# Moving layer norm's sums, differences and squares to GpSimd, in among the attention blocks of an encoder layer

## The chip, the cores and the metric

One Trainium2 chip; the kernel runs on one of its cores. The core has a matrix engine (PE, its weight loads shown as PEld), a vector engine (DVE), a scalar engine (ACT), GpSimd (POOL) and a sync engine (SP), which here only issues DMAs. Each engine works through its own queue of instructions strictly in order, and waits on semaphores for the others. The metric is the device time of one execution in microseconds (us); lower is better.

## The reference

One layer of a hybrid encoder on 512 tokens with 1024 channels, in float32. Three parts of it matter here:

```python
h = rmsnorm(x, norm1_g); z = h @ w_in               # conv input | q | k | v | two branch gates
u = a * sigmoid(b)                                  # GLU of the conv input
u = depthwise_conv31(u) + dw_b
mu = mean(u, channels); var = mean((u - mu) ** 2)   # layer norm over the 1024 channels of a token
conv_out = silu((u - mu) * rsqrt(var + EPS) * ln_g + ln_b) @ w_pw
attn_out = windowed_gqa(q, k, v, sink) @ w_o        # 16 heads, 4 key heads, blocks of 128 queries
x = x + (gate_A * conv_out + gate_B * attn_out) @ w_out
x = x + peer_ffn(rmsnorm(x))                        # top-16 of 128 x 128 experts, 8 heads
```

The last line takes most of the time (from about 500 us on), and the change doesn't touch it.

## The kernel before, in words

Activations lie with channels on the partitions: a matrix of 1024 channels by 512 tokens is eight tiles of 128x512, such as `cv[:, k, :]`, the result of the convolution. A sum over channels is therefore a sum over partitions and over the eight tiles: PE makes it by multiplying with a 128x128 matrix of 1/1024 (`ones`), eight matmuls that add up in one PSUM tile (L360 for the mean, L368 for the variance). These are plain float32 matmuls, which the profile shows as two passes each, so 16 passes for a sum.

All other matrix products run on rounded pairs. `split` (L57 to L59) makes from a float32 tile a rounded `hi` on ACT and the residual `lo = src - hi` on DVE or POOL, and `mm3` (L61 to L66) multiplies hi by hi, hi by lo and lo by hi. A weight block of 1024x128 is loaded by SP to `wraw` and split in two halves of 128x512 (`halves`, L107 to L114), into a ring of four halves. `lo_engine` says who makes the residuals: POOL for the input projection, DVE for `w_o` (L387) and `w_pw` (L425).

The stretch around the change, in order of the program:

1. The convolution (`conv`, L224 to L233) on DVE, while PE computes the input projection.
2. Attention (L350 to L355): four key heads `g` by four query blocks `b`, so 16 blocks `attend(g, b)` (L276 to L321). A block is a chain over the engines: scores on PE; mask, bias and row maximum on DVE (L290); the negated maximum `nm` (L293) and `es` (L295) on DVE; exponentials on ACT (L298, L300); the denominator `den` (L301), its reciprocal (L303) and the scaling, half of it on DVE (L308) and half on ACT (L306); transposes on PE (L313); the split of the transposed weights on ACT and DVE; the product with v on PE; and the split of its result. The projection of a branch gate (`fill`, L332) is put in behind five of the blocks, to give PE work.
3. Layer norm (L356 to L377): sum, mean, then for each tile difference (DVE, L365), square (ACT, L367) and sum (PE, L368), then square root on ACT, reciprocal on DVE (L371), scaling (DVE, L373), `Silu` on ACT (L375), split (ACT, DVE).
4. The output projection of attention, `w_o`, eight blocks of 24 matmuls (L386 to L388), then `w_pw` (L424 to L429), then `w_out` (L410 to L416), whose first half's residuals `olo` are POOL's.

The framework's scheduler writes the instructions of each engine into one fixed order, by its own costs. So parts 2 to 4 overlap: matmuls of `w_o` stand on PE between the last attention blocks, and the layer norm begins before attention ends. An engine doesn't pass over an instruction that waits.

Of the kernel before, what the change touches and what calls it, by code (L numbers as in the profile page):

```python
# [7 lines left out]
F32 = mybir.dt.float32  # L8
# [4 lines left out]
AF = mybir.ActivationFunctionType  # L13
OP = mybir.AluOpType
# [3 lines left out]
P = 128  # L18
S = 512
D = 1024  # L20
NT = S // P
KD = D // P
# [23 lines left out]
def encoder_block(ctx, tc, x, g1, w_in, taps, dwb, lng, lnb, w_pw, sink, w_o, w_out, g2, g2row,  # L46
                  w_query, keys, ut, u, v, gfin, out):
    nc = tc.nc
    ACT, DVE, POOL, PE, SP = nc.scalar, nc.vector, nc.gpsimd, nc.tensor, nc.sync
# [20 lines left out]
    ones = const.tile([P, P], F32, name="ones")  # L70
# [4 lines left out]
    epst = const.tile([P, 1], F32, name="epst")  # L75
# [42 lines left out]
    with ExitStack() as fc:  # L118
# [13 lines left out]
        cv = cpool.tile([P, KD, S], F32, name="cv")  # L132

        with ExitStack() as x0c:
# [6 lines left out]
            with tc.manual_schedule(engines=ordered):  # L141
# [15 lines left out]
                for t in range(NT):  # L157
                    rs = sm.tile([P, 1], F32, name="rs")
# [3 lines left out]
                for k in range(KD):  # L162
# [6 lines left out]
                    if k in (1, 4):  # L169
                        n = KD // 2  # L170
# [17 lines left out]
        def proj(src, rhs, ws=None, lo_engine=POOL, ps=None):  # L188
            ws = ws or weights(src, lo_engine)
            ps = psm.tile([P, S], F32, name="mm") if ps is None else ps  # L190
            mm3(ps, ws, rhs)
            return ps
# [5 lines left out]
        with ExitStack() as ac:  # L198
# [39 lines left out]
            for i in range(2):  # L238
                ps = proj(w_in[24 + i], hT)
# [5 lines left out]
            for i in range(2):  # L245
                ps = proj(w_in[26 + i], hT)
# [85 lines left out]
            def fill(n):  # L332
                for _ in range(n):
                    gate(gates.pop(0))
# [12 lines left out]
            fill(2)  # L347
            glup.close()
            pso = ac.enter_context(tc.tile_pool(name="pso", bufs=1, space=PSUM))
            for g in range(4):  # L350
                make_bias(g)
                for b in range(NT):
                    attend(g, b)
                    if b == 1 or (g, b) == (0, 3):
                        fill(1)  # L355
            lnp = ac.enter_context(tc.tile_pool(name="lnp", bufs=2))  # L356
            ac_hi, ac_lo = bigtile(), bigtile()
            mu_ps = pso.tile([P, S], F32, name="ln")
            for k in range(KD):
                PE.matmul(mu_ps, ones, cv[:, k, :], start=k == 0, stop=k == KD - 1)  # L360
            mu = lnp.tile([P, S], F32, name="rs", bufs=1)
            ACT.activation(mu, mu_ps, AF.Copy)
            var = pso.tile([P, S], F32, name="ln")
            for k in range(KD):
                DVE.tensor_tensor(cv[:, k, :], cv[:, k, :], mu, op=OP.subtract)  # L365
                sq = lnp.tile([P, S], F32, name="sq")
                ACT.activation(sq, cv[:, k, :], AF.Square)  # L367
                PE.matmul(var, ones, sq, start=k == 0, stop=k == KD - 1)  # L368
            rs = lnp.tile([P, S], F32, name="rs", bufs=1)
            ACT.activation(rs, var, AF.Sqrt, bias=epst)  # L370
            DVE.reciprocal(rs, rs)  # L371
            for k in range(KD):
                DVE.tensor_tensor(cv[:, k, :], cv[:, k, :], rs, op=OP.mult)  # L373
                act = lnp.tile([P, S], F32, name="act", bufs=2)
                ACT.activation(act, cv[:, k, :], AF.Silu, scale=vec["lng"][:, k:k + 1],  # L375
                               bias=vec["lnb"][:, k:k + 1])
                split(ac_hi[:, k, :], ac_lo[:, k, :], act, DVE)  # L377
            acT = [(ac_hi[:, k, :], ac_lo[:, k, :]) for k in range(KD)]
            oT = [(qh[:, k, :], ql[:, k, :]) for k in range(KD)]
# [4 lines left out]

            sigmoid(1)
            for j in range(KD):  # L386
                ps = proj(w_o[j], oT, lo_engine=DVE)  # L387
                DVE.tensor_tensor(sg[1][:, j, :], ps, sg[1][:, j, :], op=OP.mult)  # L388
            sigmoid(0)

# [33 lines left out]
        for j in range(KD):  # L424
            ps = proj(w_pw[j], acT, lo_engine=DVE)  # L425
# [44 lines left out]
    with ExitStack() as rc:  # L470
# [72 lines left out]
        with qc:  # L543
# [44 lines left out]
            for h in range(HP):  # L588
                scs = []
                for p in range(2):  # L590
                    n = 2 * h + p
# [272 lines left out]
```

## Time and profile before

| | us |
|---|---|
| median of 3 runs (lowest, highest) | 1784.65 (1777.46, 1793.43) |
| the profiled execution, its own time | 1791.42 |
| its span, first to last instruction | 1789.6 |
| mean granted PE clock, as a share of full speed | 0.99 |
| PE busy | 1726.0 (96%) |
| DVE busy | 1416.6 (79%) |
| ACT busy | 769.0 (43%) |
| POOL busy | 938.3 (52%) |

The busy shares are averages over stages with different limits: POOL is at 52% over the span, but it is idle for most of attention and for most of the output projections. What the change is worth has to be read in its own stretch, from about 228 us (the end of the convolution) to about 472 us (the start of `w_out`). From there on the order of the instructions is the same in both kernels, on every engine.

A busy PE in these views isn't PE at its peak: ends of matmuls are modelled, and an instruction that waits in the pipeline counts as busy. The spacing of matmuls is the better measure.

### The profile page before, as it was taken

The page shows a single profiled execution, that of the slowest core. Times are in us where ns is not written, and L with a number is a line of the kernel's source. Part 1 is how long each engine was busy: PE and PEld are TensorE (multiplying, and loading weights), DVE is VectorE, ACT ScalarE, POOL GpSimd, SP SyncE. Part 2 cuts the span into 40 slices and gives each one's busy share as a digit, 9 for nine tenths or more (in the row PEclk, how much of TensorE's full clock was granted, in tenths as well). Part 3 has the DMA queues.
Part 4 walks back from the last instruction along what each step waited for, and adds up shares of the span by engine and source line. Part 5 has one row for each costly group of instructions (what it writes and reads, how often), then busy time and mean ns, then how long its engine had stood idle before and what let it go on. Part 6 is the DMA issues. An engine that isn't in the chain of part 4 may idle for free.

```text
span 1789.6 us, 25354 instructions
## 1 busy us (share of the span) xinstructions
PE 1726.0 (96%) x8873; PEld 1487.9 (83%) x8873; DVE 1416.6 (79%) x2507; ACT 769.0 (43%) x1379; POOL 938.3 (52%) x741
## 2 busy tenths in 40 slices
PE   7999999989999979999999999999999999998998
PEld 5788876658888868998999999999999898996776
DVE  5999956674536999999668978888878798888964
ACT  4333367882343335665433334333332333332343
POOL 4444421020134444445447878888876878886401
PEclk9999999999999989999999999999999999998999
DMA  4223210034243114988788898998898889889952
GB/s 159 86 91 99 93 57 24 25 93 144 81 140 110 57 54 136 283 259 277 273 271 313 320 320 307 328 327 313 316 320 288 290 322 331 301 300 330 352 199 93
DMA packets 158159, 379.43 MB, mean 212 GB/s; under 512 B 12544, under 2 KB 64784, under 8 KB 158032
## 3 DMA queue, kind: packets, MB, share of 16 engines
q1 hardware_dynamic: 120048, 241.21, 39.0%
q0 software_dynamic: 37120, 134.52, 22.0%
q10 hardware_dynamic: 864, 2.10, 0.3%
q8 instruction: 69, 1.13, 0.3%
q14 instruction: 58, 0.48, 0.1%
HBM read 346.84 MB, written 30.93 MB: 211 GB/s over the span
## 4 chain that ended last, share of the span: by engine, by line
PE 57%; DVE 12%; DMA 11%; issue 4%; POOL 2%; ACT 2%; SPq 0%; POOLq 0%; DVEq 0%; ACTq 0%
PE acc L65 6%; PE acc L66 6%; PE acc L64 6%; PE hps L66 6%; PE hps L65 6%; PE hps L64 6%; DMA uraw<-in_ut_dram 5%; PE mm L66 5%; PE mm L64 5%; PE mm L65 5%; DMA row<-in_v_dram,eidx 4%; DMA vraw<-in_v_dram 2%; POOL row L663 1%; POOL ulo L59 1%; DVE oij L635 1%
## 5 line engine op out<-in xcount | busy, mean ns | idle before, releaser
L59 POOL TENSOR_TENSOR ulo<-uraw,uhi 128x512 fp32r<-128x512 f32 x256 | 396.3, 1560 | 297.9 <-ACT uhi L58 288.6
L64 PE MATMUL hps<-big,uhi 128*128 128x384 f32 x1024 | 348.0, 340 | 2.2 <-ACT hb L466 2.1
L66 PE MATMUL hps<-big,ulo 128*128 128x384 f32 x1024 | 348.2, 340 | 1.2 <-POOL ulo L59 1.2
L65 PE MATMUL hps<-big,uhi 128*128 128x384 f32 x1024 | 346.7, 339 | 0.0
L66 PE MATMUL acc<-vhl,pl 128*128 128x512 f32 x768 | 303.1, 395 | 10.3 <-DVE pl L59 10.3
L64 PE MATMUL acc<-vhl,ph 128*128 128x512 f32 x768 | 302.2, 393 | 4.3 <-ACT vhl L58 3.5
L65 PE MATMUL acc<-vhl,ph 128*128 128x512 f32 x768 | 302.9, 394 | 1.1 <-DVE vhl L59 0.9
L59 POOL TENSOR_TENSOR wlo<-wraw,whi 128x512 fp32r<-128x512 f32 x120 | 157.8, 1319 | 196.0 <-ACT whi L58 190.2
L670 DVE SCALAR_TENSOR_TENSOR row<-row,h2tok 128x1024 f32<-128x1024 f32 x128 | 194.0, 1516 | 62.6 <-DMA row<-in_u_dram,eidx 62.1
L681 DVE SCALAR_TENSOR_TENSOR yacc<-row,dots,yacc 128x1024 f32<-128x1024 f32 x127 | 198.8, 1566 | 50.9 <-DMA row<-in_v_dram,eidx 50.2
L58 ACT ACTIVATE vhl<-vraw 128x1024 fp32r<-128x1024 f32 x128 | 135.2, 1056 | 241.5 <-DMA vraw<-in_v_dram 234.2
L58 ACT ACTIVATE uhi<-uraw 128x512 fp32r<-128x512 f32 x256 | 156.9, 630 | 163.3 <-PE hps L65 99.8
L64 PEld LDWEIGHTS hps<-big,uhi 128*128 128x128 f32 x1024 | 193.8, 189 | 6.3 <-ACT hb L466 2.4
L65 PEld LDWEIGHTS hps<-big,uhi 128*128 128x128 f32 x1024 | 194.0, 189 | 4.0
L66 PEld LDWEIGHTS hps<-big,ulo 128*128 128x128 f32 x1024 | 193.7, 189 | 2.7 <-POOL ulo L59 2.7
L663 POOL DMA_INDIRECT row<-in_v_dram,eidx x128 | 165.4, 1292 | 56.9 <-DVE yacc L681 32.8
L58 ACT ACTIVATE whi<-wraw 128x512 fp32r<-128x512 f32 x152 | 95.1, 631 | 231.9 <-PE mm L65 127.1
L663 POOL DMA_INDIRECT row<-in_u_dram,eidx x128 | 175.3, 1369 | 31.8 <-issue 23.8
L66 PEld LDWEIGHTS acc<-vhl,pl 128*128 128x128 f32 x768 | 145.8, 190 | 44.7 <-DVE pl L59 13.8
L59 DVE TENSOR_TENSOR vhl<-vraw,vhl 128x1024 fp32r<-128x1024 f32 x128 | 160.4, 1253 | 26.3 <-ACT vhl L58 26.1
L64 PEld LDWEIGHTS acc<-vhl,ph 128*128 128x128 f32 x768 | 145.6, 190 | 32.7 <-ACT vhl L58 3.8
L65 PEld LDWEIGHTS acc<-vhl,ph 128*128 128x128 f32 x768 | 145.6, 190 | 28.9 <-DVE vhl L59 1.8
(231 smaller groups left out, 3111.4 us busy)
## 6 DMA issues: line engine op xcount, KB each, us to landing
uraw<-in_ut_dram SPq DMA_DIRECT2D x128, 512.0 KB, 6.7
vraw<-in_v_dram SPq DMA_DIRECT2D x128, 512.0 KB, 6.0
gates_dram<-st SPq DMA_DIRECT2D x12, 2048.0 KB, 8.6
gt<-gates_dram SPq DMA_DIRECT2D x96, 256.0 KB, 6.0
wraw<-in_w_in_dram SPq DMA_DIRECT2D x44, 512.0 KB, 3.3
wraw<-in_w_query_dram SPq DMA_DIRECT2D x16, 512.0 KB, 3.4
wraw<-in_w_o_dram SPq DMA_DIRECT2D x8, 512.0 KB, 3.2
oraw<-in_w_out_dram SPq DMA_DIRECT2D x16, 256.0 KB, 3.0
```

The costliest lines, as they stand in the source:

```text
L58: ACT.activation(hi, src, AF.Copy)
L59: lo_engine.tensor_tensor(lo, src, f(hi), op=OP.subtract)
L64: PE.matmul(ps, wh, mh, start=first and i == 0, stop=False)
L65: PE.matmul(ps, wh, ml, start=False, stop=False)
L66: PE.matmul(ps, wl, mh, start=False, stop=last and i == n - 1)
L635: DVE.tensor_tensor(prs(oij), iota8, rows(0), op=OP.is_equal)
L663: POOL.indirect_dma_start(out=row, out_offset=None, in_=table, in_offset=bass.IndirectOffsetOnAxis(ap=eidx[:, c:c + 1], axis=0))
L670: DVE.scalar_tensor_tensor(row, row, 1.0, h2tok, op0=OP.mult, op1=OP.mult, accum_out=dots[:, c:c + 1])
L681: DVE.scalar_tensor_tensor(yacc, row, dots[:, c:c + 1], yacc, op0=OP.mult, op1=OP.add)
```

## The change

The layer norm's sum over tiles is made on POOL (seven additions into `stat`, L360 and L362 of the new kernel), so that PE has one column sum left of eight matmuls (`colsum`); so has the variance. Difference, square and sum of squares of each tile are three POOL instructions (`ln_square`, L366 to L370), 23 in all, since the first square goes to `stat` directly. They are called behind the attention blocks: the mean behind the second block, the squares of the eight tiles behind blocks (1,0) to (2,3). The second column sum, square root, reciprocal, scaling and `Silu` stand behind attention in the program, as before. The residuals of `w_o` are made by POOL instead of DVE (16 instructions of 128x512).

```diff
@@ -347,30 +347,44 @@
             pso = ac.enter_context(tc.tile_pool(name="pso", bufs=1, space=PSUM))
+            lnp = ac.enter_context(tc.tile_pool(name="lnp", bufs=2))
+            stat = lnp.tile([P, S], F32, name="stat", bufs=1)
+            mu = lnp.tile([P, S], F32, name="mu", bufs=1)
+
+            def colsum():
+                ps = pso.tile([P, S], F32, name="ln")
+                PE.matmul(ps, ones, stat, start=True, stop=True)
+                return ps
+
+            def ln_mean():
+                POOL.tensor_tensor(stat, cv[:, 0, :], cv[:, 1, :], op=OP.add)
+                for k in range(2, KD):
+                    POOL.tensor_tensor(stat, stat, cv[:, k, :], op=OP.add)
+                ACT.activation(mu, colsum(), AF.Copy)
+
+            def ln_square(k):
+                POOL.tensor_tensor(cv[:, k, :], cv[:, k, :], mu, op=OP.subtract)
+                sq = stat if k == 0 else lnp.tile([P, S], F32, name="sq", bufs=2)
+                POOL.tensor_tensor(sq, cv[:, k, :], cv[:, k, :], op=OP.mult)
+                if k:
+                    POOL.tensor_tensor(stat, stat, sq, op=OP.add)
+
             for g in range(4):
                 make_bias(g)
                 for b in range(NT):
                     attend(g, b)
                     if b == 1 or (g, b) == (0, 3):
                         fill(1)
-            lnp = ac.enter_context(tc.tile_pool(name="lnp", bufs=2))
+                    if (g, b) == (0, 1):
+                        ln_mean()
+                    n = 4 * g + b - 4
+                    if 0 <= n < KD:
+                        ln_square(n)
             ac_hi, ac_lo = bigtile(), bigtile()
-            mu_ps = pso.tile([P, S], F32, name="ln")
+            ACT.activation(mu, colsum(), AF.Sqrt, bias=epst)
+            DVE.reciprocal(mu, mu)
             for k in range(KD):
-                PE.matmul(mu_ps, ones, cv[:, k, :], start=k == 0, stop=k == KD - 1)
-            mu = lnp.tile([P, S], F32, name="rs", bufs=1)
-            ACT.activation(mu, mu_ps, AF.Copy)
-            var = pso.tile([P, S], F32, name="ln")
-            for k in range(KD):
-                DVE.tensor_tensor(cv[:, k, :], cv[:, k, :], mu, op=OP.subtract)
-                sq = lnp.tile([P, S], F32, name="sq")
-                ACT.activation(sq, cv[:, k, :], AF.Square)
-                PE.matmul(var, ones, sq, start=k == 0, stop=k == KD - 1)
-            rs = lnp.tile([P, S], F32, name="rs", bufs=1)
-            ACT.activation(rs, var, AF.Sqrt, bias=epst)
-            DVE.reciprocal(rs, rs)
-            for k in range(KD):
-                DVE.tensor_tensor(cv[:, k, :], cv[:, k, :], rs, op=OP.mult)
+                DVE.tensor_tensor(cv[:, k, :], cv[:, k, :], mu, op=OP.mult)
                 act = lnp.tile([P, S], F32, name="act", bufs=2)
@@ -384,7 +398,7 @@
             for j in range(KD):
-                ps = proj(w_o[j], oT, lo_engine=DVE)
+                ps = proj(w_o[j], oT)
                 DVE.tensor_tensor(sg[1][:, j, :], ps, sg[1][:, j, :], op=OP.mult)
```

The scheduler's order moves with it, on PE, ACT, DVE and POOL, between the end of the convolution and `w_out`. Three places matter.

POOL from the last residuals of the input projection on (in the program: the first attention blocks; `wlo` are residuals of gate weights). Before, 43 residuals followed each other here, then the eight `olo`. In the new kernel:

```order
L59 TENSOR_TENSOR wlo<-wraw,whi 128x512 x34
L360 TENSOR_TENSOR stat<-cv 128x512
L59 TENSOR_TENSOR wlo<-wraw,whi 128x512
L362 TENSOR_TENSOR stat<-stat,cv 128x512 x5
L59 TENSOR_TENSOR wlo<-wraw,whi 128x512
L362 TENSOR_TENSOR stat<-stat,cv 128x512
L59 TENSOR_TENSOR wlo<-wraw,whi 128x512 x2
L366 TENSOR_TENSOR cv<-cv,mu 128x512 x2
L368 TENSOR_TENSOR stat<-cv 128x512
L59 TENSOR_TENSOR wlo<-wraw,whi 128x512
L368 TENSOR_TENSOR sq<-cv 128x512
L366 TENSOR_TENSOR cv<-cv,mu 128x512
```

All 30 layer-norm instructions stand in one run of the queue, with three residuals between the seven additions and the differences, and the differences wait for `mu`; the program spreads the squares over eight blocks, the scheduler does not.

ACT in the last four attention blocks. Before, this is how the end of attention and the start of `Silu` (L375) read; the square root's table load (L370) stands behind the last block's `qh<-o`:

```order
L367 ACTIVATE sq<-cv 128x512 x2
L58 ACTIVATE qh<-o 64x4x128
L367 ACTIVATE sq<-cv 128x512 x2
L58 ACTIVATE ohi_4034<-oraw 128x512
L367 ACTIVATE sq<-cv 128x512 x2
L58 ACTIVATE ohi_4040<-oraw 128x512
L58 ACTIVATE ohi_4046<-oraw 128x512
L58 ACTIVATE ohi_4052<-oraw 128x512
L370 ACT_TABLE_LOAD
L370 ACTIVATE rs<-ln,epst 128x512
```

In the new kernel the square root (L384) and `Silu` (L389) come while four blocks still have exponentials (L298) to do:

```order
L384 ACT_TABLE_LOAD
L384 ACTIVATE mu<-ln,epst 128x512
L58 ACTIVATE qh<-o 64x4x128
L298 ACT_TABLE_LOAD
L298 ACTIVATE L,den<-L,nm 128x256 x4
L300 ACTIVATE es<-es 128x4
L58 ACTIVATE whi<-wraw 128x512 x3
L306 ACTIVATE L<-L,rd 128x256 x2
L389 ACT_TABLE_LOAD
L389 ACTIVATE act<-cv,lnb,lng 128x512
L58 ACTIVATE ph<-pt 128x512 x2
L298 ACT_TABLE_LOAD
```

This alternation of L298 and L389, each with a table load, goes on to the last block. Seven table loads stand here ahead of the last `qh<-o`; before, two stood in the same blocks, around one of the two large sigmoids (L383), which in the new kernel comes behind the last block.

DVE in the same blocks, in the new kernel (`L387` is the scaling, L373 before, of which all eight stood behind attention):

```order
L387 TENSOR_TENSOR cv<-cv,mu 128x512
L308 TENSOR_SCALAR L<-L,rd 128x384 x2
L290 ISA L,m<-s,bias,sinkt 128x256
L290 ISA m 128x1
L290 ISA L,m<-s,bias,sinkt 128x256
L290 ISA m 128x1
L387 TENSOR_TENSOR cv<-cv,mu 128x512
L59 TENSOR_TENSOR pl<-pt,ph 128x512 x2
L301 TENSOR_TENSOR den<-den,es 128x4
L293 TENSOR_SCALAR nm<-m 128x4
L295 TENSOR_TENSOR es<-sinkt,m 128x4
```

The reciprocal of 128x512, all eight scalings and four of the eight splits of `act` stand ahead of the last block's end, in between the blocks' own instructions. Seven of the eight subtractions that stood there before (L365) are gone.

## Rows read from the trace of the kernel before

**Rows 1.** The page: shares of the chain that ended last, by engine.
```profile
PE 57%; DVE 12%; DMA 11%; issue 4%; POOL 2%; ACT 2%; SPq 0%; POOLq 0%; DVEq 0%; ACTq 0%
```

**Rows 2.** Stretches (us): length, then busy us (instructions) of each engine.
```profile
core 0: us, PE busy (x) PEld busy (x) DVE busy (x) ACT busy (x) POOL busy (x), PEclk, DMA share, GB/s
237.00:285.00 48.00, 47.87 (x231) 34.49 (x229) 31.48 (x101) 35.85 (x96) 7.75 (x6) 1.00 0.11 33
345.00:378.00 33.00, 30.64 (x139) 21.08 (x138) 24.55 (x66) 29.40 (x71) 0.00 (x0) 1.00 0.04 12
378.00:400.00 22.00, 17.10 (x62) 11.26 (x62) 16.77 (x22) 18.56 (x30) 10.53 (x8) 0.99 0.56 165
400.00:428.00 28.00, 28.00 (x116) 22.60 (x116) 12.38 (x20) 9.07 (x15) 0.00 (x0) 0.95 0.54 188
```

**Rows 3.** Waits of PE, 225 to 480 us: in total, times, longest.
```profile
PE mm L64 <- DVE sg L388: 3.9, 2, 2.2
PE mm L66 <- DVE wlo L59: 1.0, 1, 1.0
```

**Rows 4.** Chain of waits, 325 to 380 us: start, us, what (column sums).
```profile
328.44 1.72 PE ln L360 x4
...
373.41 1.72 PE ln L368 x4
```

**Rows 5.** Tile `ln`: passes, ns min/median/max, first and last start.
```profile
L360 PE MATMUL ln<-cv,ones x16: 592/593/697, 328.3 to 344.6; 128*128 128x512 f32 x16
...
L368 PE MATMUL ln<-sq,ones x16: 592/592/697, 373.2 to 381.8; 128*128 128x512 f32 x16
```

**Rows 6.** Groups, 100 to 480 us: count | busy us, mean ns | idle before.
```profile
L59 POOL TENSOR_TENSOR wlo<-wraw,whi 128x512 fp32r<-128x512 f32 x56 | 72.5, 1295 | 114.7 <-ACT whi L58 113.3 <-PE s L66 1.4
...
L59 DVE TENSOR_TENSOR pl<-pt,ph 128x512 fp32r<-128x512 f32 x40 | 26.2, 685 | 18.1 <-ACT ph L58 18.1
...
L59 DVE TENSOR_TENSOR wlo<-wraw,whi 128x512 fp32r<-128x512 f32 x32 | 21.7, 686 | 9.2 <-ACT whi L58 9.2
...
L383 ACT ACTIVATE sg<-sg 128x4096 f32<-128x4096 f32 x2 | 7.2, 3625 | 0.0
...
L375 ACT ACTIVATE act<-cv,lnb,lng 128x512 f32<-128x512 f32 x8 | 6.1, 807 | 1.6 <-DVE big L59 1.6
...
L367 ACT ACTIVATE sq<-cv 128x512 f32<-128x512 f32 x8 | 4.7, 628 | 0.5 <-PE ln L368 0.5
L58 ACT ACTIVATE big<-act 128x512 fp32r<-128x512 f32 x8 | 4.5, 616 | 0.0
...
L298 ACT ACT_TABLE_LOAD x3 | 3.8, 1283 | 0.0
...
L371 DVE RECIPROCAL rs<-rs 128x512 f32<-128x512 f32 x1 | 3.4, 3354 | 5.2 <-ACT rs L370 5.2
```

**Rows 7.** Timeline of DVE near 249 and 390 us: start us, us, what.
```profile
248.89 1.77 DVE L308 TENSOR_SCALAR L<-L,rd 128x384 f32<-128x384 f32 x2
389.94 1.78 DVE L373 TENSOR_TENSOR cv<-cv,rs 128x512 f32<-128x512 f32 x1
```

**Rows 8.** Timeline of POOL at the same places.
```profile
249.04 1.40 POOL L59 TENSOR_TENSOR wlo<-wraw,whi 128x512 fp32r<-128x512 f32 x1 [10.71 <-ACT whi L58]
388.20 2.96 POOL L59 TENSOR_TENSOR olo<-oraw,ohi 128x512 fp32r<-128x512 f32 x2
```

**Rows 9.** Groups of DVE, 237 to 285 us.
```profile
L290 DVE CUSTOM_DVE_ANT_0 L<-s,bias,sinkt 128x256 f32<-128x256 f32 (+1 forms) x24 | 12.6, 546 | 15.7 <-PE s L66 15.6
...
L308 DVE TENSOR_SCALAR L<-L,rd 128x256 f32<-128x256 f32 (+1 forms) x12 | 5.2, 469 | 0.2
...
L293 DVE TENSOR_SCALAR nm<-m 128x4 f32<-128x4 f32 x6 | 1.7, 278 | 0.1
...
L301 DVE TENSOR_TENSOR den<-den,es 128x4 f32<-128x4 f32 x6 | 1.0, 160 | 1.6 <-ACT es L300 1.6
L295 DVE TENSOR_TENSOR es<-sinkt,m 128x4 f32<-128x4 f32 x6 | 0.9, 155 | 0.0
```

## The prediction

> **What bounds the kernel now.** The page's chain of waits comes first: more than half of what ended last is PE [rows 1], so an edit counts as far as it shortens or lengthens PE's queue. The shares are averages, so the next view is the table of stretches around the change [rows 2]. Between 237 and 285 us, with the first attention blocks, PE is busy throughout, DVE and ACT for about two thirds, and POOL for 7.75 of 48 us. From 345 to 378 us, with the last four blocks, ACT is busy for 29.4 of 33 us and PE begins to have gaps. From 378 to 400 us, at the end of the layer norm, PE has 4.9 us of gaps. Third, PE's waits [rows 3] say what these last ones are: 3.9 us for `sg` (L388), which on DVE stands behind the reciprocal and the scalings, and 1.0 us for a residual of `w_o`. Last, the chain in order of time [rows 4] shows that PE's column sums stand on it: they are no filler.
>
> **PE, removed.** Two sums of 16 passes [rows 5]. Four passes take 1.72 us on the chain [rows 4], 0.43 each, so 32 take 13.8 us; the new ones need two matmuls, four passes, 1.7 us. That is **-12.1 us**, and all of it is on the path: PE is the engine waited for at both places.
>
> **PE, waits behind the layer norm's end.** Reciprocal and scalings now come before attention ends, and the residuals of `w_o` leave DVE's queue. The two waits of [rows 3] go: **-4.9 us**. What would be late next is `w_o`'s residuals on POOL, 16 of 1.295 us [rows 6], or 20.7 us, together with eight `olo`, 31 us; `w_o`'s 192 matmuls, at the 28 us for 116 of PE's instructions from 400 to 428 us [rows 2], hold PE for 46 us, and `olo` is first read behind `w_o` and `w_pw`. SP's loads of `w_pw` now stand behind loads of `w_out` that wait for those `olo`; the same stretch of matmuls hides it. If the cover were gone, each late half would cost PE up to 1.295 us.
>
> **POOL, added in attention.** 30 instructions of 128x512. Nearest row: POOL's residuals, two inputs from SBUF and the same size, 1.295 us [rows 6], so 38.9 us. The queue starts the additions when the convolution ends, at about 228 us, has seven residuals among or just before the layer norm's 30, and waits once for the mean: 37 instructions end at 276 us without that wait, at about 285 us with it. The second column sum stands on PE behind the last gate projection, after 328 us, where the old sums begin [rows 5]. So POOL has some 40 us in hand, and its duration costs nothing by itself.
>
> What does cost is DVE beside it. [Rows 7, 8]: two L308 with a POOL residual running took 1.77 us together, where the other ten take (5.2 - 1.77) / 10 = 0.34 each [rows 9]; the scaling at 389.94 us took 1.78 us, where 0.69 is its size [rows 6], and it ended 0.55 us behind POOL's `olo`, which ended at 391.17. These instructions didn't share with POOL, they waited for its end. A DVE instruction with an operand in PSUM did not wait: the 40 `pl` took 685 ns each [rows 6]. In a block five instructions have all operands in SBUF: `nm`, `es`, `den` and two L308. From 237 to 285 us there are 6, 6, 6 and 12 of them [rows 9]. POOL will be busy for some 38 of these 48 us, a share of 0.8. An instruction that arrives at random waits half a POOL instruction, 0.65 us times 0.8, and 18 of them (`nm`, `den`, the first L308) make 9.4 us; the 12 that follow such a one (`es`, the second L308) find the next POOL instruction in front of them, as at 249 us, and wait 1.295 times 0.8: 12.4 us. Less the 1.7 us that L308 and `nm` lose there already, DVE gets 20 us more. It was busy for 31.5 of 48 us and would need 51.5. The least that reaches PE is therefore 3.5 us, the most 20. DVE waits 15.7 us there for scores [rows 9]; I let two thirds of it soak up the new waits, not all, since within a block DVE, ACT and PE take turns. I take **+9 us**.
>
> [...]
>
> **ACT and DVE, moved into the last four blocks.** The removed column sums let the scheduler put the layer norm's end among blocks that ACT already fills. ACT: seven table loads for two, 5 x 1.283 = +6.4 us; four `Silu` at 0.807, +3.2; four copies of `act` at 0.616, +2.5; one sigmoid goes behind the blocks, -3.6; four squares go, -2.5 [rows 6]. Net +6.0 on 29.4 of 33 us [rows 2]. DVE: the reciprocal, +3.35; eight scalings and four splits at 0.686, +8.2; seven subtractions and two residuals less, -6.2 [rows 6]. Net +5.4 on 24.6 us. POOL's `w_o` residuals run there too: two of DVE's instructions behind them, +2.6. If all of it is serial, which the chain of a block nearly is, +14; the least is what ACT can't hold, 35.4 less 33, +2.4. With few blocks left there is little to overlap with; I take **+13 us**.
>
> **Nothing** for the moved copy of the mean on ACT (0.6 us, it was there before) and for the five gate residuals behind POOL's run: the ring of four halves has them ready about a block ahead; if not, PE waits for gate matmuls that other work could have replaced, up to 1.3 us each.
>
> **The sum** is -12.1 - 4.9 + 9 + 13 = **+5 us** on an execution of 1791.4 us. That one lies 6.8 us above the median of the runs shown and inside their spread, so I carry the difference over: 1784.65 + 5 = **1790 us**. One per cent, about what a measurement of this kernel can tell from no change, is 17.8 us: all that the change removes, 17.0 us, is just below it.
>
> **Rivals.**
> - *The cover holds.* DVE's idle time soaks up all it can and the last blocks overlap: -17.0 + 3.5 + 2.4 = -11, **1774 us**. For it: DVE had 16.5 idle us in the first stretch. Against: a block's chain has `nm`, `den` and L308 in series. 0.20.
> - [...] DVE needs 51.5 of 48 us between 237 and 285, and from the point at which its queue has no gap left each wait for POOL moves scores, and with them PE, one for one: -17.0 + 20 + 14 = +17, and a PE that then waits in the last blocks falls to the lower of its clocks more often: the granted 0.95 behind the gaps before 400 us [rows 2] cost 1.4 of 28 us, and twice that makes +20, **1805 us**. Slower. For it: waits in the chain of a block add up. Against: two blocks run interleaved. 0.15.
> - *POOL itself is the bound.* [...] [Rows 6] give 1.295 against 0.686 us for the same residual. POOL's run would have to end 43 us later than 285 us to hold up the second column sum; if it did, by waiting for DVE as DVE waits for it, each us beyond would be one on PE: with ten beyond, **1800 us**. 0.04.
> - *No trace of it.* The scheduler's order leaves the gains and losses as they are, and nothing of either reaches the end, because the later stages wait for something else: 1785 us. Against: the chain is PE's from end to end. 0.03.
>
> My forecast gets 0.58. Its own range is 1781 to 1798 us.
>
> **Numbers.** Faster by over 1% needs nearly the whole gain and no loss, a small part of the first rival: 0.04. Slower by over 1% is most of the second and a part of the third, with the upper edge of the forecast: 0.17. Within 1%: 0.79. For 8 in 10 the range takes in the first rival and the second up to its middle: **1774 to 1803 us**.
>
> **What would show it.** Column sums of four passes instead of 32. POOL busy for over 35 us between 237 and 285 us; L293, L295, L301 and L308 longer there by a total of 15 us or more, `pl` unchanged. The first blocks ending about 9 us later, and the last attention product, with about 24 of the old 32 passes gone ahead of it (-10 us), about 12 us later than before. Twelve ACT table loads for seven up to there, and no wait of PE for L402 (`sg`) or `wlo` over 1 us. `w_out` starting at about 477 us for 472. I am wrong if the last attention product comes earlier than before, if DVE's five instructions keep their old durations, or if `w_o` waits for POOL.

## The result, and the profile after

| | before | the change |
|---|---|---|
| median of 4 runs each (lowest, highest), us | 1788.77 (1777.46, 1793.43) | 1808.36 (1802.56, 1812.53) |
| ratio, 95% interval | 1 | 1.0123 [1.0086, 1.0159] |
| end of the 4th, 12th, 16th attention block, us | 273.7, 352.1, 376.6 | 295.8, 365.1, 410.3 |
| first product of `w_out` on PE, us | 471.7 | 496.6 |

The change is slower, by 1.0123 x 1785 - 1785 = 22 us; that makes 1807 us, outside the forecast range (1774 to 1803). The ratios here and below compare runs of both kernels on one chip and aren't quotients of the medians (here 1808.36 / 1788.77 = 1.011); one run of t1 below is left out of its ratio, since it took 3430.7 us. Blocks are told by the start of the copy of their result on ACT (`qh`). The start of `w_out` is the mark for all kernels below, since the same work follows in all of them. The spans are not a good one: from that product to the start of the last instruction the profiled run of before took 1313.6 us, that of the change 1302.0, with the same work in it. The delay of that mark, 24.9 us, is near what the ratio gives.

The page's chain of the changed kernel says less than it seems:
```profile
PE 45%; DVE 15%; DMA 15%; issue 8%; POOL 4%; ACT 2%; SPq 1%; POOLq 0%; DVEq 0%; ACTq 0%
```
PE lost 12 points against [rows 1], but to whom, and where, only the stretches tell. They answer to [rows 2] (length, then busy us of each engine; a number in brackets counts instructions):
```profile
core 0: us, PE busy (x) PEld busy (x) DVE busy (x) ACT busy (x) POOL busy (x), PEclk, DMA share, GB/s
238.00:265.00 27.00, 24.92 (x115) 17.43 (x114) 19.92 (x52) 16.08 (x44) 17.34 (x16) 1.00 0.11 39
265.00:281.00 16.00, 1.24 (x6) 0.68 (x4) 16.00 (x3) 0.52 (x1) 15.96 (x14) 0.65 0.00 0
281.00:328.00 47.00, 45.33 (x213) 33.28 (x214) 28.63 (x93) 35.08 (x93) 7.65 (x6) 0.94 0.08 23
328.00:361.00 33.00, 32.95 (x154) 22.48 (x153) 21.53 (x66) 27.93 (x63) 1.27 (x1) 1.00 0.05 17
361.00:377.00 16.00, 10.69 (x41) 7.60 (x41) 14.96 (x29) 14.30 (x28) 4.22 (x3) 0.74 0.11 34
377.00:389.00 12.00, 12.00 (x30) 7.81 (x28) 6.93 (x21) 6.78 (x19) 0.00 (x0) 0.50 0.00 0
389.00:410.00 21.00, 13.79 (x64) 8.65 (x62) 12.35 (x29) 18.78 (x39) 0.17 (x1) 0.99 0.00 0
410.00:453.00 43.00, 41.80 (x168) 33.13 (x169) 11.84 (x16) 24.63 (x34) 24.34 (x19) 0.93 0.61 208
```
Two rows stand out. From 265 to 281 us PE does 1.24 us of work and ACT 0.52, while DVE is "busy" for all 16 us with 3 instructions. From 377 to 389 us PE is busy throughout, but with 30 matmuls in 12 us, at a granted clock of 0.50. [Rows 2] have nothing like either; the lowest clock there is 0.95, with 0.50 from 400 to 402 us in it.

DVE's timeline names the instruction (start us, us, what); POOL's own beside it:
```profile
260.19 1.33 DVE L293 TENSOR_SCALAR nm<-m 128x4 f32<-128x4 f32 x1
261.43 1.33 DVE L295 TENSOR_TENSOR es<-sinkt,m 128x4 f32<-128x4 f32 x1
...
264.99 16.00 DVE L293 TENSOR_SCALAR nm<-m 128x4 f32<-128x4 f32 x1
280.91 0.15 DVE L295 TENSOR_TENSOR es<-sinkt,m 128x4 f32<-128x4 f32 x1
```
```profile
264.94 1.29 POOL L370 TENSOR_TENSOR stat<-stat,sq 128x512 f32<-128x512 f32 x1
266.20 1.03 POOL L368 TENSOR_TENSOR sq<-cv 128x512 f32<-128x512 f32 x1
...
279.93 1.03 POOL L368 TENSOR_TENSOR sq<-cv 128x512 f32<-128x512 f32 x1
281.04 1.26 POOL L370 TENSOR_TENSOR stat<-stat,sq 128x512 f32<-128x512 f32 x1
```
At 260 and 261 us `nm` and `es` (0.17 and 0.15 us of work) last 1.33, one POOL instruction each, as forecast. At 265 us `nm`, 0.17 us of work, lasts 16.00: 14 POOL instructions end while it waits. Each starts 0.03 to 0.04 us before its predecessor ends, and then comes one that doesn't: the addition at 281.04 reads the square that ended at 280.96, so POOL pauses for 0.08 us, and there `nm` ends. The waits from 238 to 283 us (in total, times, longest) show who hung on it; of PE's waits before, [rows 3] shows the longest, 2.2 us:
```profile
ACT L L298 <- DVE nm L293: 19.8, 4, 15.5
PE pt L313 <- DVE L L308: 16.7, 2, 16.4
```
The forecast's four groups of DVE, from 237 us to the end of the fourth block (count, then busy us, mean ns):
```profile
L293 DVE TENSOR_SCALAR nm<-m 128x4 f32<-128x4 f32 x5 | 19.0, 3808 | 0.1
L308 DVE TENSOR_SCALAR L<-L,rd 128x256 f32<-128x256 f32 (+1 forms) x8 | 4.5, 601 | 0.1
L295 DVE TENSOR_TENSOR es<-sinkt,m 128x4 f32<-128x4 f32 x5 | 3.1, 620 | 0.0
L301 DVE TENSOR_TENSOR den<-den,es 128x4 f32<-128x4 f32 x4 | 0.6, 159 | 0.7 <-ACT es L300 0.7
```
Together they last 27.2 us; the same 22 instructions of before last 6.7. The 20.5 us more are the 20 of the forecast, but by luck: one instruction makes up 15.8 of them.

PE's column sums did become four passes (count, then ns min/median/max, first and last start), for 32 in [rows 5], and ACT loads tables 12 times before `w_out`, as forecast:
```profile
L356 PE MATMUL ln<-stat,ones x4: 590/591/595, 250.6 to 349.4; 128*128 128x512 f32 x4
```

### The profile page after: what moved, and what is told of

It reads as the page before. It is cut to its first block, busy times and chain, and to the rows that moved or that the text cites. A ratio compares the mean times of both kernels' runs of the same rounds, so it can differ in the third digit from the quotient of the medians.

```text
span 1803.3 us, 25321 instructions
## 1 busy us (share of the span) xinstructions
PE 1721.8 (95%) x8845; PEld 1488.0 (83%) x8845; DVE 1419.3 (79%) x2483; ACT 776.9 (43%) x1376; POOL 1000.5 (55%) x787
## 4 chain that ended last, share of the span: by engine, by line
PE 45%; DVE 15%; DMA 15%; issue 8%; POOL 4%; ACT 2%; SPq 1%; POOLq 0%; DVEq 0%; ACTq 0%
DMA uraw<-in_ut_dram 6%; PE mm L65 5%; PE mm L64 5%; PE mm L66 5%; DMA row<-in_v_dram,eidx 4%; PE acc L66 4%; PE acc L65 4%; PE acc L64 4%; PE hps L64 4%; PE hps L65 4%; PE hps L66 4%; DMA row<-in_u_dram,eidx 3%; POOL row L677 3%; POOL ulo L59 2%; DVE yacc L695 2%
## 5 line engine op out<-in xcount | busy, mean ns | idle before, releaser
L59 POOL TENSOR_TENSOR ulo<-uraw,uhi 128x512 fp32r<-128x512 f32 x256 | 391.4, 1544 | 254.9 <-ACT uhi L58 237.8
L59 POOL TENSOR_TENSOR wlo<-wraw,whi 128x512 fp32r<-128x512 f32 x136 | 178.7, 1319 | 288.3 <-ACT whi L58 278.6
L684 DVE SCALAR_TENSOR_TENSOR row<-row,h2tok 128x1024 f32<-128x1024 f32 x128 | 207.7, 1623 | 57.1 <-DMA row<-in_u_dram,eidx 56.6
L695 DVE SCALAR_TENSOR_TENSOR yacc<-row,dots,yacc 128x1024 f32<-128x1024 f32 x127 | 192.9, 1519 | 43.8 <-DMA row<-in_v_dram,eidx 42.0
L677 POOL DMA_INDIRECT row<-in_u_dram,eidx x128 | 185.1, 1446 | 31.7 <-issue 27.2
L58 ACT ACTIVATE ph<-hb 128x384 fp32r<-128x384 f32 (+1 forms) x132 | 67.3, 513 | 253.2 <-PE acc L65 243.0
L64 PEld LDWEIGHTS acc<-vhl,ph 128*128 128x128 f32 x768 | 144.7, 188 | 31.9 <-ACT vhl L58 4.0
```

The source lines that it names most:

```text
L58: ACT.activation(hi, src, AF.Copy)
L59: lo_engine.tensor_tensor(lo, src, f(hi), op=OP.subtract)
L64: PE.matmul(ps, wh, mh, start=first and i == 0, stop=False)
L677: POOL.indirect_dma_start(out=row, out_offset=None, in_=table, in_offset=bass.IndirectOffsetOnAxis(ap=eidx[:, c:c + 1], axis=0))
L684: DVE.scalar_tensor_tensor(row, row, 1.0, h2tok, op0=OP.mult, op1=OP.mult, accum_out=dots[:, c:c + 1])
L695: DVE.scalar_tensor_tensor(yacc, row, dots[:, c:c + 1], yacc, op0=OP.mult, op1=OP.add)
```

## Experiments

Theories at the start. **A**: some 14 us are DVE passed over by an unbroken run of POOL. **B**: the rest is the end of the layer norm among the last four blocks. **Rival**: the residuals of `w_o` on POOL, or POOL's total load. All shifts below are against the profiled run of before, in us; ratios are against runs of before on the same chip. Every shift is read from one profile; e2, t1 and v2, whose edits touch nothing up to the fourth block, give +0.5 to +0.8 there, so a shift under 1 us says nothing.

| kernel | 4th block | 12th | 16th | `w_out` | ratio [95%] |
|---|---|---|---|---|---|
| the change | +22.1 | +13.0 | +33.7 | +24.9 | 1.0123 [1.0086, 1.0159] |
| e1_ln_only | +20.6 | +12.3 | +31.3 | +22.3 | 1.0134 [1.0067, 1.0201] |
| e2_wo_only | +0.5 | -0.2 | +2.5 | +5.1 | 1.0031 [1.0000, 1.0063] |
| e3_chained | +7.6 | -1.5 | +19.4 | +10.2 | 1.0070 [1.0038, 1.0101] |
| e4_end_behind | +25.5 | +16.4 | +25.9 | +24.6 | 1.0129 [1.0087, 1.0170] |
| e5_both | +10.6 | +1.5 | +12.0 | +11.4 | 1.0073 [1.0052, 1.0095] |
| e6_both_dve | +7.3 | -1.0 | +9.5 | +5.4 | 1.0064 [1.0040, 1.0089] |
| s1_long | +25.3 | +16.3 | +37.2 | +28.0 | one run, 1814.7 us |
| s2_gap | +9.1 | +0.1 | +20.2 | +10.6 | 1.0081 [1.0048, 1.0113] |
| t1_no_sums | +0.5 | -7.0 | +7.6 | -1.7 | 0.9983 [0.9961, 1.0006] |
| v1_sig | +12.9 | +4.9 | +8.7 | +4.3 | 0.9999 [0.9979, 1.0019] |
| v3_spread | +2.5 | -5.1 | +0.4 | -4.0 | 0.9981 [0.9950, 1.0012] |
| v2_sig_before | +0.8 | -4.7 | +0.8 | -1.1 | 0.9983 [0.9953, 1.0013] |

**The two parts apart.**
```diff
-                ps = proj(w_o[j], oT)                     # e1: in the change
+                ps = proj(w_o[j], oT, lo_engine=DVE)
-                ps = proj(w_o[j], oT, lo_engine=DVE)      # e2: in the kernel before
+                ps = proj(w_o[j], oT)
```


> The layer norm's part alone: sums, differences and squares on POOL as in the change, the residuals of w_o on DVE as before. Theory A (one VectorE instruction is passed over by POOL's unbroken layer-norm run for 16 us): the long L293 is here too, 10 us or longer, the first three or four blocks end about 20 us later than before, and the time is 1.006 to 1.014 of before's, most of the change's 1.012. Rival (the residuals of w_o on POOL are what costs, by meeting VectorE's scalings in the last blocks): the time is within 0.4% of before's.

> The other part alone: residuals of w_o on POOL, the layer norm as before. Theory A: attention up to 340 us stands as before to within 1 us, and the time is 0.997 to 1.003 of before's. Rival (the residuals are what costs): 1.005 to 1.012.

The layer norm's part carries the loss (1.0134; L293 lasts 16.01 us here too). The residuals alone are no gain either: +5.1 us at `w_out`, though taking them out of the change (e1) moves that mark by only 2.6. Of the waits that I had struck out, the larger grew from 3.9 us [rows 3] to 7.0 in e2, since `sg` on DVE stands behind scalings that now wait for POOL (seven of them take 9.27 us there, 1.32 each, for 0.69 without such a wait):
```profile
PE mm L64 <- DVE sg L388: 7.0, 2, 5.8
```

**POOL's order.** e3 only fixes the order of POOL's instructions: difference, square, addition of one tile, then the next, so that two of three read what the one just ahead wrote.
```diff
-                POOL.tensor_tensor(cv[:, k, :], cv[:, k, :], mu, op=OP.subtract)
+                chain(POOL.tensor_tensor(cv[:, k, :], cv[:, k, :], mu, op=OP.subtract))
...   # the square and the addition likewise; chain() queues each behind the one before, without a wait
```


> The change, but POOL's layer norm in the order difference, square, addition of one tile and then the next, so that square and addition each read what the instruction just ahead of them on POOL has written; same instructions, same number. Theory A: POOL has a short gap at each such step and VectorE gets in; the longest wait of a 128x4 instruction is under 4 us instead of 16.0, the first four blocks end 3 to 10 us later than before instead of 22, and the time is 10 to 20 us below the change's (ratio to before 1.001 to 1.007). Rival (POOL's total load, or the sum of many single waits, delays the blocks): blocks still about 20 us late, time as the change's 1.012.

The rows of L293 and L308 (ns min/median/max) of e3, 238 to 290 and 287 us:
```profile
L293 DVE TENSOR_SCALAR nm<-m x6: 165/185/1266, 240.2 to 286.6; 128x4 f32<-128x4 f32 x6
...
L308 DVE TENSOR_SCALAR L<-L,rd x10: 345/744/1436, 244.7 to 286.3; 128x256 f32<-128x256 f32 x6, 128x384 f32<-128x384 f32 x4
```
The longest L293 is 1.27 us for 16.00, and the blocks lose 7.6 us for 22.1, with the same 30 POOL instructions in 52.7 us for 52.0. Theory A holds for some 14 us of the 22. What makes up the other 7.6 this run doesn't show; the four groups of DVE last 6.8 us longer in e3 than before (13.5 for 6.7), and PE's granted clock was 0.89 in e3 from 266 to 282 us, for 1.00 before [rows 2]. By the ratios the step is smaller, 0.0053 or 9 us, with intervals that overlap; the profile shows which instruction it is.

**POOL and DVE by themselves.**
```diff
+            for k in range(n):
+                POOL.tensor_tensor(dst, src, a[:, S:S + width], op=OP.add)
+                if k == 1:
+                    ACT.activation(trig, dst[:, :1], AF.Copy)
+            for k in range(6):
+                DVE.tensor_scalar(r[:, :w], src[:, :w], trig, None, op0=OP.mult)
```


> Nothing of the encoder is computed here: only nine sections, in each of which POOL runs 16 (or 32) additions of 128x512 with all operands in SBUF and VectorE six small instructions of 128x4 that become ready once the second addition has ended. Theory A: with additions that don't depend on one another (sections 1 and 2) the first VectorE instruction waits for nearly the whole run, about 17 us with 16 additions and 37 us with 32; where each addition reads the one just ahead (section 3) it waits for one or two additions, 1.3 to 2.6 us; where it reads the one two or three ahead (4, 5) the semaphore is already there and the wait is long again. With the small operand in PSUM (6) it waits for nothing. With 32 additions of 128x256 (7) the wait is again the run, about 19 us. With VectorE's six of 128x512 (8, 9) the same as with small ones. Rival (the two take turns): one addition, 1.3 us, in every section with SBUF operands.

Theory A failed here. Groups of DVE (busy us, mean ns); `triga` to `trige` are sections 1 to 5, `trigf` has its operand and result in PSUM:
```profile
L79 DVE TENSOR_SCALAR rFalse<-m,trigc 128x4 f32<-128x4 f32 x6 | 7.6, 1270 | 3.2 <-ACT trigc L74 3.0
L79 DVE TENSOR_SCALAR rFalse<-m,trigb 128x4 f32<-128x4 f32 x6 | 6.9, 1148 | 3.1 <-ACT trigb L74 2.9
...
L79 DVE TENSOR_SCALAR rTrue<-mp,trigf 128x4 f32<-128x4 f32 x6 | 1.4, 230 | 3.1 <-ACT trigf L74 2.9
```
In an unbroken run of 32 additions (39.04 us without an idle stretch) each small instruction lasts 1.15 us, about one addition, and gets in, although POOL never pauses; in PSUM it lasts 0.23 and waits for none. Where the additions read the one two or three ahead (sections 4 and 5) it is 1.15 too. So an unbroken run doesn't by itself shut DVE out. This wait of about one addition is what the next expectation calls the lock.

**Is it the moment of arrival?**
```diff
+            DVE.tensor_scalar(d[:, :w], s[:, :w], trig, None, op0=OP.mult)   # w sets the shift
+            DVE.tensor_tensor_reduce(L, s, bias, 0.125, sink[:, :1], OP.add, OP.max, m[:, :1])
+            DVE.tensor_scalar(nm, m, -1.0, None, op0=OP.mult)
```


> Nothing of the encoder is computed: 66 sections in a row. In the first 40 POOL runs the 23 layer-norm instructions in the change's order while VectorE does a reduction as L290, a 128x4 as L293 and a 128x4 as L295, with VectorE's start shifted by about 12 ns from section to section; then 16 sections with 20 equal additions on POOL (shifts of 33 ns), then 10 with the layer norm in the chained order (52 ns). The first bare measurement showed turns, one POOL instruction per VectorE instruction, so what made the 16 us is open. Theory A1 (it takes the layer norm's own order and a certain moment of arrival): among the first 40 some 128x4 last over 5 us, in a narrow band of shifts, the others 0.15 to 1.4 us; none among the last 26. Theory A2 (it takes the moment alone): also among the 16 with equal additions. Rival (the lock is not it, something else in the change held L293): none of the 66 lasts over 2 us.

> Nothing of the encoder is computed: 50 sections as in the earlier bare measurement (40 with the layer norm in the change's order, 10 in the chained order), now with VectorE coming twice to the same run of POOL, the second time with L290 four times, L293 and two more 128x4, shifted by about 12 ns per section, and with ScalarE busy beside it. Theory A4 (the long wait comes only for a VectorE that has already waited once in this run, with ScalarE's work beside it): in the change's order some second L293 last 5 us or more; in the chained order none lasts over 2 us. Rival (it takes something else of the real kernel): none of the 50 lasts over 2 us, as in the earlier 66.

None of the 116 did it: the longest are 1.28 and 1.31 us.
```profile
L112 DVE TENSOR_SCALAR nm<-m x66: 170/1022/1279, 14.1 to 1770.1; 128x4 f32<-128x4 f32 x66
```
```profile
L126 DVE TENSOR_SCALAR nm<-m x50: 170/356/1314, 16.1 to 1366.4; 128x4 f32<-128x4 f32 x50
```
The rivals hold: what first makes DVE miss its turn is something of the real kernel that these don't have. What ends the wait can be tested there.

**What ends the wait.** s1 lengthens the run behind the place, s2 puts one pause into it; no other engine's order changes.
```diff
                     POOL.tensor_tensor(stat, stat, sq, op=OP.add)
+                    if k >= 4:                                              # s1
+                        POOL.tensor_tensor(extra, cv[:, k, :], mu, op=OP.add)
...
+                if k >= 4:                                                  # s2: order alone
+                    behind(diff, adds[3] if k == 4 else sqs[4])
```


> The change with four more additions on POOL (into a tile that nobody reads) between the squares of tiles 4 to 7; nothing else moves, and up to the third addition the order is the change's. Theory A3 (VectorE, once passed over, gets in only when POOL pauses because an instruction reads what the one just ahead of it writes): the first such pause comes now between the last difference and its square, so the long L293 lasts about 19 us. Rival (a fixed time): 16.0 us as in three runs before. Rival (chance): under 3 us.

> The change with one step moved on POOL: the difference of tile 4 behind the third addition, so that this addition reads what the square just ahead of it writes; every other instruction on every engine stands as in the change. Theory A3: L293 meets a pause after some 2.3 us in place of 16.0; blocks 3 to 12 end 10 to 14 us earlier than in the change unless a later VectorE instruction is passed over again, and the time is 8 to 14 us below the change's (ratio to before 1.004 to 1.009). Rival (POOL's total load delays the blocks): as the change, 1.012.

DVE in s1, and POOL at the place where it ends:
```profile
265.20 18.66 DVE L293 TENSOR_SCALAR nm<-m 128x4 f32<-128x4 f32 x1
```
```profile
282.56 1.27 POOL L367 TENSOR_TENSOR cv<-cv,mu 128x512 f32<-128x512 f32 x1
283.91 1.04 POOL L369 TENSOR_TENSOR sq<-cv 128x512 f32<-128x512 f32 x1
```
The wait is 18.66 us, not 16, and ends at 283.86, 0.03 us behind the difference of 282.56, whose square waits for it: at POOL's first pause. In s2 the long wait is gone and the gain is what A3 expects (1.0081, 13.0 us less than the change at the 12th block), but in detail not as expected: `nm`, which came 0.06 us behind the start of an addition as in the change (0.05), got in at that addition's end, one instruction before the pause.
```profile
264.06 1.27 DVE L293 TENSOR_SCALAR nm<-m 128x4 f32<-128x4 f32 x1
265.24 1.08 DVE L295 TENSOR_TENSOR es<-sinkt,m 128x4 f32<-128x4 f32 x1
```

**The last four blocks.** e4 pins the square root, and with it all that follows, behind the last attention block on ACT; e5 does that with e3's order, e6 also has `w_o`'s residuals on DVE.
```diff
-            ACT.activation(mu, colsum(), AF.Sqrt, bias=epst)
+            tc.keep_in_program_order(ACT.activation(mu, colsum(), AF.Sqrt, bias=epst))
```


> The change with the end of the layer norm (square root, and with it reciprocal, scalings, Silu, splits) pinned behind the last attention block's instructions on ScalarE. Theory B (this end among the last four blocks is what makes them longer): the last block ends as much later than before as the fourth one does (about 21 us, less the column sums that are gone: 10 to 15 us later than before; 34 in the change), and the time is 12 to 20 us below the change's, ratio to before 1.000 to 1.006. Rival (the blocks are late because of w_o's residuals on POOL or because PE's clock fell): the last block still 28 us late or more, ratio 1.010 to 1.014.

> Chained order on POOL and the end of the layer norm pinned behind attention, residuals of w_o on POOL. Theories A and B together: blocks 4 to 12 are 0 to 8 us late, the last block 0 to 5 us early, start of w_out 0 to 8 us earlier than before, ratio to before 0.994 to 1.000. Rival as for the run before: the last block 15 us late, ratio 1.005 to 1.009.

> As the run before, with the residuals of w_o on VectorE as before the change. The run with these residuals alone cost 5 us, so theory: 3 to 6 us below the run before, ratio 0.991 to 0.998, below both kernels. Rival (VectorE's queue is fuller behind attention with scalings and these residuals, and PE waits for sg and wlo again, 4.9 us): no better than the run before.

Theory B fell. The last four blocks do get shorter (from the 12th to the 16th 45.2 us in the change, 33.9 in e4), but `w_out` starts no earlier and the ratio stays: what the end costs among the blocks it costs behind them. And they are still 9 us longer than before's 24.5. e5 and e6 stay above the ratios expected of them (1.0073 and 1.0064), and e6 is no better than e5 beyond the intervals. The stretches of e6 show what is left:
```profile
345.00:361.00 16.00, 15.97 (x70) 10.43 (x70) 11.88 (x40) 15.25 (x29) 0.00 (x0) 1.00 0.08 30
361.00:365.00 4.00, 2.38 (x9) 1.83 (x10) 3.22 (x12) 2.76 (x9) 0.00 (x0) 0.88 0.05 18
365.00:377.00 12.00, 9.05 (x28) 6.09 (x26) 4.77 (x12) 8.33 (x24) 0.00 (x0) 0.50 0.00 0
```
PE first has a gap (2.38 of 4 us), then 12 us at 0.50. Before, with the column sums in the program, the clock was 1.00 there [rows 2]. **Theory C**: the sums filled PE's gaps, and without them the clock falls.

**The sums alone, and the gap alone.** t1 takes the kernel before and leaves out seven of the eight matmuls of each sum; v1 takes e6 and moves the second sigmoid of the gates (3.62 us of ACT and two table loads, in front of that gap) behind `w_o`'s splits.
```diff
-            for k in range(KD):                                             # t1
-                PE.matmul(mu_ps, ones, cv[:, k, :], start=k == 0, stop=k == KD - 1)
+            PE.matmul(mu_ps, ones, cv[:, KD - 1, :], start=True, stop=True)
...   # var likewise
-            sigmoid(0)                                                      # v1
+            tc.keep_in_program_order(sigmoid(0))
```


> The kernel before with one matmul for eight in each of the two column sums (the sums then leave out seven tiles); everything else is computed. My sum gave PE's 32 passes 12.1 us for 28 of them, all on the path. If that term is right: start of w_out 10 to 14 us earlier, ratio 0.992 to 0.995. Theory C (they filled gaps of PE among the last blocks, and without them PE's clock falls there): start of w_out at most 5 us earlier, a stretch of granted clock 0.5 between 340 and 385 us, ratio 0.997 to 1.003.

> Chained order, end of the layer norm behind attention, residuals of w_o on VectorE, and now also the second sigmoid of the gates behind w_o's splits on ScalarE instead of among the last blocks (two table loads and 3.6 us of ScalarE, after which PE's clock fell to 0.5 for 12 us in the run without it). Theory C (the gap on PE behind that sigmoid is what drops the clock): no stretch at 0.5 among the last blocks, last block 8 to 14 us earlier than there, start of w_out at 464 to 470 us for 471.7 before, ratio 0.994 to 0.999. Rival (the last blocks lose PE's clock anyway, since their chain leaves PE idle): start of w_out above 474 us, ratio 1.002 to 1.006.

Stretches of t1, and of v1:
```profile
345.00:349.00 4.00, 3.71 (x16) 2.41 (x15) 3.50 (x15) 4.00 (x13) 0.00 (x0) 1.00 0.02 4
349.00:361.00 12.00, 11.74 (x39) 8.71 (x38) 7.78 (x27) 7.62 (x21) 0.00 (x0) 0.51 0.00 1
...
377.00:389.00 12.00, 7.04 (x15) 4.57 (x16) 11.66 (x16) 11.90 (x14) 2.11 (x2) 0.62 0.27 89
```
```profile
361.00:365.00 4.00, 4.00 (x20) 2.47 (x18) 2.56 (x10) 2.84 (x8) 0.00 (x0) 1.00 0.31 95
365.00:377.00 12.00, 10.18 (x50) 6.89 (x50) 9.34 (x31) 9.81 (x27) 0.00 (x0) 1.00 0.16 56
```
In t1 the blocks are 7.0 us early at the 12th and 7.6 late at the 16th, and `w_out` starts 1.7 us earlier: 28 passes of 0.43 us gone, 12 us of PE, are worth 1.7 us. What Theory C forecast came, with one limit: the scheduler also moved other work in t1, so this prices the removal as a kernel would get it, not the passes in place. The second sigmoid went from 341.7 us to 377.1, in among the last blocks. And the sums themselves hardly stand there: before, 16 of their passes end ahead of the 12th block, and 5 start between it and the 16th. Without them, matmuls of `w_o` stand in their place: between the fourth and the 12th block 5 before and 13 in t1, among the last four blocks 19 before and 12 in t1 (11 or 12 in the change, e5, e6 and v1). So the last blocks lack filler, but of `w_o` more than of the sums. That this lets the clock fall is argued, not shown, and it isn't all: in v1 PE stays at 1.00 with 11 of these matmuls, and the stretch from the 12th to the 16th block is 28.3 us for e6's 35.0.

But `w_out` started at 476.0 us in v1, the rival's figure, for another reason than the rival's: the first blocks lost 12.9 us there, with the same order on POOL, for 7.3 in e6. From 278 to 286 us the two read, v1 first:
```profile
278.00:286.00 8.00, 8.00 (x24) 5.96 (x23) 4.13 (x12) 2.47 (x5) 7.45 (x7) 0.50 0.00 0
```
```profile
278.00:286.00 8.00, 8.00 (x36) 5.59 (x36) 6.14 (x20) 5.11 (x16) 7.41 (x7) 1.00 0.00 1
```
In v1 one `den` lasted 1.29 us at 272 us, for 0.28 in e6; PE was busy for 2.47 of the 4 us from 274 on, for 3.66 in e6, and then did 24 matmuls in 8 us at a granted 0.50 where e6 did 36 at 1.00. So what the first blocks lose holds lost clock as well as waits. The change shows the same behind its long wait: 0.50 from 282 to 286 us.

**A better version?** v3 is v1 with each tile's three POOL instructions waiting for the last scaling of one block, the fifth to the twelfth; v2 is the kernel before with the sigmoid moved, as control.
```diff
+                tc.add_manual_dep(diff.ins, scaled[k + 4].ins.name, Sync ...)   # v3
...
-            sigmoid(0)                                                          # v2
+            tc.keep_in_program_order(sigmoid(0))
```


> As the last version (end of the layer norm behind attention, residuals of w_o on VectorE, second sigmoid behind w_o's splits), with the layer norm's three POOL instructions of a tile made to wait for the last scaling of one attention block each, from the fifth block to the twelfth, instead of following each other between 250 and 282 us. Theory A (POOL's run beside the first blocks costs 7 to 13 us there): the first four blocks end within 3 us of before's, the third to the twelfth lose under 5 us, start of w_out at 464 to 472 us for 476.0 in the last version, ratio to before 0.992 to 0.998: below both kernels. Rival (each POOL instruction costs VectorE the same wherever it stands): the blocks lose the 7 to 13 us later, ratio 0.998 to 1.002.

> The kernel before with nothing changed but the second sigmoid of the gates, which is pinned behind w_o's splits on ScalarE. It tells whether what the last versions win is the sigmoid's alone. Theory C: in the kernel before this sigmoid stands where the column sums and w_o's matmuls hide it, PE's clock stays at 1.00 there, so moving it gives little: ratio 0.997 to 1.002. Rival (it costs there too): 0.990 to 0.995.

v3 loses 2.5 us in the first blocks, with the clock at 1.00 from 258 to 294 us, and no more later: the 7 to 13 us come from the run's place. By the two ratios it is 1.4% below the change. But 0.9981 and 0.9983 can't be told from each other, nor from 1: nothing here shows a gain of the layer norm on POOL over the kernel before.

## Why the prediction was wrong

- **The step that failed first: "DVE waits for POOL", +9 us, at most 20.** It let each exposed instruction wait for at most one POOL instruction. One L293 waited for 14, and the term measured 22. The bound of 20 summed over the 30 instructions what one of them nearly cost. Without that one (e3, s2) the first blocks lose 7.6 and 9.1 us, which looks like the +9 but comes about otherwise: the four groups of DVE last only 6.8 and 10.3 us longer there, not 20, and the blocks lose about as much. That DVE's idle time soaks up some 10 us of the waits shows nowhere, and PE's granted clock in the same stretch (0.50 from 282 to 286 us in the change, 0.89 from 266 to 282 us in e3) wasn't in the term.
- **The second: "the column sums, -12.1 us, all of it on the path".** Four passes for 32 came, but the removal is worth 1.7 us (t1), since the last four blocks then take 39.1 us for 24.5. "They are no filler" was read from the chain of waits. With them in the program 19 matmuls of `w_o` stood among the last blocks and PE's clock was 1.00; without them 12 do, with stretches at 0.51 and 0.62. How much of that loss is clock, gaps or the sigmoid's move stays open. (The forecast also had 24 of the old passes gone ahead of the last attention product; it was 16, since 12 of the second sum stood behind it.)
- **Waits behind the layer norm's end, -4.9 us.** PE's wait for `sg` is gone in the change, and from the last product of attention to `w_out` it takes 87.2 us for 95.6, 8.4 less. But that is the end of the layer norm, which the last blocks now hold: e4 has it behind them, and the ratio is the same. The residuals of `w_o` on POOL, in my sum a part of this gain, cost 5.1 us alone.
- **ACT and DVE in the last four blocks, +13 us.** The size was near: from the 12th to the 16th block e3 takes 45.3 us with the end among the blocks and e5 34.9 with it behind them, 10.4 less. But it was counted as a loss against a gain of 4.9, where the same work costs as much behind the blocks (`w_out` starts 10.2 us late in e3, 11.4 in e5). And the term didn't see that the blocks without this work are 10.4 us longer than before's 24.5, with 0.50 among their clocks.
- **The sum by the runs**: +22 for DVE's waits for POOL (14 of it by one instruction), -2 for the sums, about 0 for the end of the layer norm, +5 for the residuals, +25 together, against +24.9 at `w_out`. That it comes out so closely is partly luck: the residuals are 5.1 us alone, but 2.6 within the change. The rival of 1805 us came near the time, but by many waits, not by one.

## What to carry to other kernels

Before work goes to POOL beside a chain of short VectorE instructions, look at POOL's order: here instructions that depended on one another two or three places back ran without a pause, and one VectorE instruction waited for 14 of them. Putting each behind the one that it reads (in the change and s1 POOL pauses for 0.08 us at such a step) cost POOL 52.7 us for 52.0 in all, and the longest wait was 1.27 us for 16.00 (e3); spreading them over the blocks (v3) left 2.5 us of loss. Work on PE that stands in the chain of waits may still be filler: before counting its removal as a gain, look at the granted clock (0.51 and 0.62 in two stretches of t1, for 1.00 before), and at which other work will be drawn forward into its place and be missing later (12 matmuls of `w_o` among the last blocks of t1, for 19).

## What the runs showed of the hardware

- A VectorE instruction of 0.17 us lasted 16.00, 16.01, 16.01 and 18.66 us in four kernels with the same order up to that point (the change, e1, e4, s1), in the change and s1 to POOL's first pause, of 0.08 us; in s2, with the same order up to the next POOL instruction, it lasted 1.27. In 116 bare sections it never lasted over 1.31. What decides it is open.
- PE's granted clock was 0.50 for 12 us in e6 behind four us in which PE was busy for 2.38, and 0.51 for 12 us in t1 behind four with 3.71 busy and 16 matmuls. Such 12 us hold 28 matmuls in e6, 30 in the change and 39 in t1, for 50 at 1.00 in v1; the mixes differ, and e6's PE also waits for 3 of the 12. The size of a gap alone doesn't tell: before, PE was busy for 2.89 of four us with 14 matmuls, and the clock stayed at 1.00 up to 378 us [rows 2]:
```profile
362.00:366.00 4.00, 2.89 (x14) 1.87 (x14) 2.32 (x7) 3.92 (x12) 0.00 (x0) 1.00 0.00 0
```
